# Expert weights split three loads ahead into four buffers, with a light turn's small work tied behind those splits

## The chip, the cores and the metric

One core of a Trainium2 chip runs the whole kernel in one launch. The metric is the device time of that launch in microseconds: 2012.52 us in the median of three runs before the change (2011.22 to 2013.28).

## What is computed

Two layers over 256 latent and 256 context tokens of 1024 features, in float32: a gated linear recurrence with a dense SwiGLU, then windowed attention with a mixture of experts. The change lies in the experts (and touches the attention before them):

```python
logits = (h @ router).astype(jnp.float32)
top_logit, top_idx = lax.top_k(logits, 2)                   # 2 of 8 experts a token
top_w = jax.nn.softmax(top_logit, axis=-1)
gates = jnp.sum(one_hot(top_idx, 8) * top_w[..., None], axis=-2)
for e in range(8):                                          # D_EXPERT = 3584
    g, u = jnp.split(h @ w_gate_up[e], 2, axis=-1)
    out = out + gates[..., e:e + 1] * ((silu(g) * u) @ w_down[e])
```

## The kernel before

A float32 product is made of float32r products: every operand is split into a high and a low part, `split_into` (L112, L113): ACT copies the high part to float32r, then DVE (in places POOL) subtracts it and writes the low part. `mm3` (L127 to L129) multiplies high by high, low by high and high by low.

The experts are worked off one by one, eight **turns** in an order by their number of tokens. Odd turns are **light**: at most 64 tokens, whose high and low parts stand side by side in 128 columns, so that two products for each block of weights do (L1189, L1190); `fold` (L1227) adds the two halves afterwards. Even turns are **heavy**: up to 128 tokens, three products a block. Each turn has 7 **chunks** of 512 hidden features, and a chunk 6 **loads** of weights of 1024 KB: four for gate and up (`up`), two for down (`down`). A load goes through a raw buffer (`raw`, L104: DMA on the SP queue), is split (`weights`) into one `whi` and one `wlo` buffer, and is used by PE. Heavy chunks have 72 large products, light ones 48. The buffers of a kind are used in turn. At the experts there are 11 raw buffers (4 of the stream, 5 of the pool `early`, which the attention also uses as scratch, 1 of the pool `late`, 1 in the free half of `x`) and 3 each of `whi` and `wlo`.

The loop in `run` asks for the gate and up products of a chunk, then for the down products of the chunk before; between the two down loads, `turned` brings this chunk's activations into the layout that its down products need. In a light chunk that is: ACT copies the gate sums and the up sums out of their banks (L1215), PE folds and turns them (L1227), ACT takes the silu (L1229), DVE multiplies (L1230), and the result is split (`eahi`, L112, L113). Each call of `weights` stands where its products are asked for; a scheduler puts the instructions of each engine in an order from that, and each engine works its own queue strictly in order. After a turn, `finished` scales and splits its two sums, and `scatter` adds them to the output (L1266 to L1268); `gather` makes the next turn's tokens (L1137, L1158 for a light turn, L1169 to L1181 for a heavy one).

Ahead of the experts lies the attention's out-projection, whose four loads (`swout`) and one of the experts' first two are split in quarters by ACT and POOL.

## Time and profile before

| | |
|---|---|
| runs, median (range) | 2012.52 us (2011.22 to 2013.28) |
| profiled execution | 2011.05 us, of which the span 2009.3 us |
| mean granted TensorE clock | 0.982 |
| busy: PE, DVE, ACT, POOL | 93%, 76%, 55%, 9% |
| HBM read | 477.10 MB, 238 GB/s over the span |
| experts | from about 980 us to the end |

Busy shares are of one execution. PE's products overlap each other, so that it counts as busy while its rate may be below its best. A row of waits names who waited for whom; idle time of an engine that nobody waits for costs nothing. A window gives what each engine did in a stretch of time.

### The profile page before, as it was taken

To read this page: it belongs to the slowest core of one execution; us is meant where nothing else is said; L and a number is where in the kernel's file an instruction comes from. 1 tells how busy PE (TensorE), PEld (TensorE's weight loads), DVE (VectorE), ACT (ScalarE), POOL (GpSimd) and SP (SyncE) were. 2 spreads that over 40 slices of the span, in tenths; PEclk is the share of its full clock that TensorE was granted. 3 is DMA by queue.
4 is the path that set the end of the run, shared out by engine and by line. 5 is a ranking of instruction groups with operands and counts; after the bars stand their busy time and mean duration, and the time that the engine had idled before them with its cause. 6 is when DMAs were issued, how large, how long until landed. Compare 5 with 4: busy or idle time off the path is not lost.

```text
span 2009.3 us, 29618 instructions
## 1 busy us (share of the span) xinstructions
PE 1874.9 (93%) x11580; PEld 1513.5 (75%) x11580; DVE 1522.9 (76%) x2053; ACT 1114.8 (55%) x1321; POOL 174.3 (9%) x166
## 2 busy tenths in 40 slices
PE   7999999999999999899999988998889988899877
PEld 5888878898888889667878776886668866678655
DVE  4786778596684747775598978888778887788877
ACT  3433332442122224565677877677767767677766
POOL 2233233000000000532100000000000000000000
PEclk8999999999999999898999999999999999999999
DMA  7322223555353432242499999999889999899983
GB/s 267 137 74 96 90 101 127 192 228 188 129 225 128 155 118 75 105 171 104 168 356 351 367 373 342 348 343 342 332 330 348 350 343 338 326 340 353 345 335 118
DMA packets 73811, 480.14 MB, mean 239 GB/s; under 512 B 8768, under 2 KB 11456, under 8 KB 18752
## 3 DMA queue, kind: packets, MB, share of 16 engines
q1 hardware_dynamic: 73664, 478.18, 63.5%
q8 instruction: 93, 1.52, 0.3%
q14 instruction: 54, 0.44, 0.1%
HBM read 477.10 MB, written 1.05 MB: 238 GB/s over the span
## 4 chain that ended last, share of the span: by engine, by line
PE 26%; DVE 13%; ACT 5%; DMA 5%; issue 4%; POOL 0%; DVEq 0%; ACTq 0%
DVE wlo L113 10%; PE ps_a L128 5%; PE ps_a L129 5%; PE ps_a L127 5%; ACT whi L112 4%; DMA raw<-moed 2%; DMA raw<-moegu 2%; PE ps_a L1190 2%; PE ps_b L129 2%; PE ps_b L128 2%; PE ps_b L127 2%; PE ps_a L1189 1%; DVE acc L1268 1%; PE ps_a L1158 1%; PE ps_c L1234 0%
## 5 line engine op out<-in xcount | busy, mean ns | idle before, releaser
L113 DVE TENSOR_TENSOR wlo<-raw,whi 128x2048 fp32r<-128x2048 f32 (+2 forms) x389 | 817.5, 2121 | 143.0 <-ACT whi L112 136.7
L112 ACT ACTIVATE whi<-raw 128x2048 fp32r<-128x2048 f32 (+2 forms) x421 | 703.3, 1690 | 302.6 <-PE ps_a L128 207.0
L129 PE MATMUL ps_a<-hhi,wlo 128*128 128x512 f32 (+1 forms) x800 | 283.8, 355 | 2.1 <-POOL wlo L113 2.1
L127 PE MATMUL ps_a<-hhi,whi 128*128 128x512 f32 (+1 forms) x800 | 283.4, 357 | 0.8 <-ACT hhi L112 0.7
L128 PE MATMUL ps_a<-hlo,whi 128*128 128x512 f32 (+1 forms) x800 | 283.3, 355 | 0.0
L128 PE MATMUL ps_a<-wlo,hhi 128*128 128x512 f32 (+1 forms) x720 | 256.0, 356 | 9.2 <-DVE wlo L113 9.2
L127 PE MATMUL ps_a<-whi,hhi 128*128 128x512 f32 (+1 forms) x720 | 256.3, 356 | 2.3 <-ACT hhi L359 2.0
L129 PE MATMUL ps_a<-whi,hlo 128*128 128x512 f32 (+1 forms) x720 | 253.9, 353 | 2.4 <-DVE hlo L361 2.4
L1190 PE MATMUL ps_a<-wlo,hhi 128*128 128x512 f32 x448 | 186.9, 417 | 46.5 <-DVE wlo L113 46.4
L1189 PE MATMUL ps_a<-whi,hhi 128*128 128x512 f32 x448 | 178.4, 400 | 3.9 <-ACT whi L112 3.9
L129 PEld LDWEIGHTS ps_a<-hhi,wlo 128*128 128x128 f32 x800 | 152.4, 190 | 23.3 <-POOL wlo L113 2.9
L127 PEld LDWEIGHTS ps_a<-hhi,whi 128*128 128x128 f32 x800 | 151.6, 190 | 22.8 <-ACT hhi L112 1.1
L128 PEld LDWEIGHTS ps_a<-hlo,whi 128*128 128x128 f32 x800 | 152.5, 191 | 19.4
L128 PEld LDWEIGHTS ps_a<-wlo,hhi 128*128 128x128 f32 x720 | 136.7, 190 | 31.7 <-DVE wlo L113 14.3
L127 PEld LDWEIGHTS ps_a<-whi,hhi 128*128 128x128 f32 x720 | 136.7, 190 | 25.4 <-issue 2.9
L1190 PEld LDWEIGHTS ps_a<-wlo,hhi 128*128 128x128 f32 x448 | 85.6, 191 | 88.8 <-DVE wlo L113 72.9
L129 PEld LDWEIGHTS ps_a<-whi,hlo 128*128 128x128 f32 x720 | 136.3, 190 | 19.8 <-DVE hlo L361 2.9
L219 DVE SCALAR_TENSOR_TENSOR junk<-raw,crow 128x1024 f32<-128x1024 f32 x80 | 97.7, 1221 | 33.2 <-DMA raw<-wmod1t 32.0
L1189 PEld LDWEIGHTS ps_a<-whi,hhi 128*128 128x128 f32 x448 | 85.8, 191 | 22.1 <-ACT whi L112 6.4
L1190 PE MATMUL ps_b<-wlo,eahi 128*128 128x512 f32 x224 | 85.1, 417 | 16.0 <-DVE wlo L113 15.4
L128 PE MATMUL ps_b<-wlo,eahi 128*128 128x512 f32 x224 | 88.9, 397 | 1.1 <-DVE wlo L113 1.1
L129 PE MATMUL ps_b<-whi,ealo 128*128 128x512 f32 x224 | 87.5, 392 | 0.2 <-DVE ealo L113 0.2
(379 smaller groups left out, 2906.1 us busy)
## 6 DMA issues: line engine op xcount, KB each, us to landing
raw<-moegu SPq DMA_DIRECT2D x202, 1024.0 KB, 6.7
raw<-moed SPq DMA_DIRECT2D x98, 1024.0 KB, 6.9
raw<-wmod SPq DMA_DIRECT2D x26, 1024.0 KB, 5.0
raw<-ffgu SPq DMA_DIRECT2D x22, 1024.0 KB, 4.9
raw<-wmod1t SPq DMA_DIRECT2D x20, 1024.0 KB, 4.8
x<-moegu SPq DMA_DIRECT2D x20, 1024.0 KB, 6.1
raw<-whead SPq DMA_DIRECT2D x14, 768.0 KB, 4.4
x<-moed SPq DMA_DIRECT2D x10, 1024.0 KB, 5.1
```

Of the source, the lines that this page charges most:

```text
L112: self.nc.scalar.activation(hi[:, at], x[:, at], AF.Copy)
L113: (by or self.nc.vector).tensor_tensor(lo[:, at], x[:, at], hi[:, at].bitcast(F32), op=ALU.subtract)
L127: mm(out, l[0], r[0], start=first, stop=False)
L128: mm(out, l[0], r[1], start=False, stop=False)
L129: mm(out, l[1], r[0], start=False, stop=last)
L219: nc.vector.scalar_tensor_tensor(self.junk, w[:, b], 1.0, self.crow[:, who], op0=ALU.mult, op1=ALU.mult, accum_out=self.mod[1][:, 2 * c + ...
L1158: nc.tensor.matmul(g[:, d], l[:, d], r[:, :LIGHT], start=(n == 0), stop=(n == 3))
L1189: nc.tensor.matmul(out, l, r[0], start=first, stop=False)
L1190: nc.tensor.matmul(out, l, r[1], start=False, stop=last)
L1268: nc.vector.scalar_tensor_tensor(acc[:, i, cols], o, gate[:, i, e:e + 1], acc[:, i, cols], op0=ALU.mult, op1=ALU.add)
```

## The change

1. `feed` makes one list of all loads of a run in the order of their use (`chunks`). `take` brings up the list until four loads have been asked for that are not used yet (`ahead=3`), so that three loads beyond the present one have had DMA and split asked for, and hands out the oldest. The first chunk of the first run goes without (`ahead` 0).
2. `split_into` remembers its last two instructions (`made`). `after(n)` ties what is issued in it behind the ACT half of the n-th load ahead, `after(n, True)` behind the DVE half. A light chunk's two copies and its silu come behind the third split ahead, the product of gate and up behind the first, the split of the result behind the third (ACT) and the second (DVE).
3. The last three of these, `finished` and `gather` are kept in a list (`later`), which is worked off within the next `up` behind the first load's products. `folded`, with the fold on PE, comes behind both down loads.
4. Buffers: `early` has 4 instead of 5, `late` is gone, so 9 raw buffers; `whi` and `wlo` have 4 each.
5. In a heavy chunk the silu of the gate sums is asked for before the up products, not after.

```diff
-            self.more(self.pool(self.ctx, "early"), raw=5)
+            self.more(self.pool(self.ctx, "early"), raw=4)
...
-            self.slots["raw"] += [(self.pool(es, "late"), 1), (None, 1)]
-            self.more(self.pool(es, "ahead"), whi=1, wlo=1)
+            self.slots["raw"] += [(None, 1)]
+            self.more(self.pool(es, "ahead"), whi=2, wlo=2)
...
+                def take(ahead=3):
+                    for name, k, at, pieces in islice(todo, max(0, ahead + 1 - len(ready))):
+                        src = ins[name][(FIRST,) + at] if k == 0 else ins[name][(bass.ds(number[k], 1),) + at][0]
+                        with nullcontext() if ahead else tc.issue_after(self.gathered):
+                            ready.append(self.weights(src, 2048, pieces=pieces, loads=pieces) + self.made)
+                    return ready.pop(0)[:2]
+
+                def after(n, low=False):
+
+                    return tc.issue_after(ready[n][2 + low]) if n < len(ready) else nullcontext()
...
                 for j in range(2):
                     for kh in range(2):
-                        ...
-                                w = self.weights(source("moegu", k, c, j, kh), 2048, pieces=at, loads=at)
-                        w = [t.rearrange("p (k n) -> p k n", k=4) for t in w]
+                        w = [t.rearrange("p (k n) -> p k n", k=4) for t in self.take(ahead)]
                         ...
+                        while later:
+                            later.pop(0)()
+                    if light:
+                        with self.after(2):
+                            nc.scalar.copy(out[j], gu[j])
+                    elif j == 0:
+                        nc.scalar.activation(out[0], gu[0], AF.Silu)
...
+            def folded(both):
                 ...
+                with self.after(2):
+                    nc.scalar.activation(a, g, AF.Silu)
+
+                def later():
+                    with self.after(0, True):
+                        nc.vector.tensor_tensor(a, u, a, op=ALU.mult)
+                    with self.after(2):
+                        nc.scalar.activation(out[:, :, :LIGHT], a, AF.Copy)
+                    with self.after(1, True):
+                        nc.vector.tensor_tensor(out[:, :, LIGHT:], a, out[:, :, :LIGHT].bitcast(F32), op=ALU.subtract)
+                return out, later
...
-                        down(pe, pc, pact, y, (0,))
-                        if e < NE:
+                        down(pc, pact, y, (0,))
+                        if e < NE and not light:
                             act = turned(act)
-                        down(pe, pc, pact, y, (1,))
+                        down(pc, pact, y, (1,))
+                        if e < NE and light:
+                            act, rest_of = folded(act)
+                            later.append(rest_of)
```

**ACT, a chunk of a light turn.** Before: the chunk whose gate sums are ps_a_12616 and up sums ps_a_12617. Its loads are 12619 and 12633 (gate), 12647 and 12661 (up); 12677 and 12705 are the down loads of the chunk before.

```order
L112 ACTIVATE whi_12633<-raw_12631 128x2048
L112 ACTIVATE whi_12647<-raw_12645 128x2048
L1215 COPY x_76<-ps_a_12616 128x512
L112 ACTIVATE whi_12661<-raw_12659 128x2048
L112 ACTIVATE whi_12677<-raw_12675 128x2048
L1215 COPY x_76<-ps_a_12617 128x512
L112 ACTIVATE whi_12705<-raw_12703 128x2048
L1229 ACTIVATE x_76<-ps_c_12689 128x256
L112 ACTIVATE whi_12721<-raw_12719 128x2048
L112 ACTIVATE eahi_12690<-x_76 128x4x64
```

After: gate sums ps_a_12625 of the loads 12573 and 12588, up sums ps_a_12626 of 12602 and 12629; 12646 and 12661 are the down loads of the chunk before, 12674, 12689 and 12703 the first loads of the next chunk.

```order
L114 ACTIVATE whi_12629<-raw_12627 128x2048
L1269 ACTIVATE eahi_12615<-x_76 128x4x64
L114 ACTIVATE whi_12646<-raw_12644 128x2048
L1236 COPY x_76<-ps_a_12625 128x512
L114 ACTIVATE whi_12661<-raw_12659 128x2048
L114 ACTIVATE whi_12674<-x_76 128x2048
L1236 COPY x_76<-ps_a_12626 128x512
L114 ACTIVATE whi_12689<-raw_12687 128x2048
L114 ACTIVATE whi_12703<-raw_12701 128x2048
L1263 ACTIVATE x_76<-ps_c_12715 128x256
```

The copy of the gate sums stood one split beyond the last gate load and stands three beyond; so does the copy of the up sums (one beyond 12661 before; 12646, 12661 and 12674 beyond 12629 after).

**PE, the same chunks.** Before, around the fold of the gate sums, within the products of the first up load (ps_a_12617):

```order
L1190 MATMUL ps_a_12616<-wlo_12634,hhi_91 128x512
L1189 MATMUL ps_a_12617<-whi_12647,hhi_91 128x512
L1227 MATMUL ps_c_12689<-fold_9527,x_76 128x64 x4
L1190 MATMUL ps_a_12617<-wlo_12648,hhi_91 128x512
L1189 MATMUL ps_a_12617<-whi_12647,hhi_91 128x512
L1190 MATMUL ps_a_12617<-wlo_12648,hhi_91 128x512
```

After, from the last product of the up sums on; ps_b are the sums of the down products of the chunk before:

```order
L1218 MATMUL ps_a_12626<-wlo_12630,hhi_91 128x512
L1217 MATMUL ps_a_12626<-whi_12629,hhi_91 128x512
L1218 MATMUL ps_a_12626<-wlo_12630,hhi_91 128x512
L1217 MATMUL ps_b_12483<-whi_12646,eahi_12615 128x512
L1217 MATMUL ps_b_12484<-whi_12646,eahi_12615 128x512
L1260 MATMUL ps_c_12715<-fold_9525,x_76 128x64 x4
L1218 MATMUL ps_b_12483<-wlo_12647,eahi_12615 128x512
```

The fold moved from the first up load to the first down load of the chunk before, two loads later.

**POOL, the end of the attention.** L826 and L828 (after: L829, L831) are the two steps of a query norm, of the third and the fourth group of heads here; wlo rows are quarters of weight splits: first eight of the queries' weights, later those of the out-projection and of one load of the experts (four of them before from the buffer in `x`). Before:

```order
L113 TENSOR_TENSOR wlo<-raw,whi 128x512 x8
L826 TENSOR_TENSOR raw<-raw,cst 128x512
L828 TENSOR_TENSOR raw<-raw 128x512
L826 TENSOR_TENSOR raw<-raw,cst 128x512
L828 TENSOR_TENSOR raw<-raw 128x512
L113 TENSOR_TENSOR wlo<-raw,whi 128x512 x8
L113 TENSOR_TENSOR wlo<-x,whi 128x512 x4
L113 TENSOR_TENSOR wlo<-raw,whi 128x512 x8
```

After:

```order
L115 TENSOR_TENSOR wlo<-raw,whi 128x512 x8
L829 TENSOR_TENSOR raw<-raw,cst 128x512
L831 TENSOR_TENSOR raw<-raw 128x512
L115 TENSOR_TENSOR wlo<-raw,whi 128x512 x6
L829 TENSOR_TENSOR raw<-raw,cst 128x512
L115 TENSOR_TENSOR wlo<-raw,whi 128x512
L831 TENSOR_TENSOR raw<-raw 128x512
L115 TENSOR_TENSOR wlo<-raw,whi 128x512 x13
L1027 TENSOR_TENSOR hlo<-yn,hhi 128x4x128
```

Seven quarters of the out-projection's splits moved ahead of the last step of the fourth norm.

## Rows read from the trace of the kernel before

**Rows 1.** The page: busy time of the engines over the whole span (share, instructions).

```profile
PE 1874.9 (93%) x11580; PEld 1513.5 (75%) x11580; DVE 1522.9 (76%) x2053; ACT 1114.8 (55%) x1321; POOL 174.3 (9%) x166
```

**Rows 2.** Instructions of DVE in order of time, the additions of a turn's sums to the output: start us, us, instruction, count. Those after the first and the second turn.

```profile
1129.70 2.73 DVE L1268 SCALAR_TENSOR_TENSOR acc<-ps_a,gate,acc 128x512 f32<-128x512 f32 x4
1254.30 2.72 DVE L1268 SCALAR_TENSOR_TENSOR acc<-ps_a,gate,acc 128x512 f32<-128x512 f32 x4
```

**Rows 3.** Windows between the starts of these additions: stretch, its length, then busy us (instructions) of PE, PEld, DVE, ACT, POOL, the granted clock, DMA share, GB/s. In order: first light turn, second heavy, fourth turn (light), third heavy, sixth turn (light), fourth heavy, last light turn with the end.

```profile
1129.70:1254.30 124.60, 109.68 (x507) 85.51 (x506) 106.61 (x72) 93.83 (x84) 0.00 (x0) 0.97 0.91 356
1254.30:1377.00 122.70, 118.28 (x547) 95.34 (x546) 105.03 (x67) 89.25 (x69) 0.00 (x0) 1.00 0.93 345
1377.00:1513.70 136.70, 114.19 (x520) 86.72 (x520) 109.51 (x73) 96.93 (x85) 0.00 (x0) 0.99 0.87 337
1513.70:1636.00 122.30, 117.89 (x545) 95.01 (x544) 104.59 (x67) 89.08 (x69) 0.00 (x0) 1.00 0.93 344
1636.00:1773.00 137.00, 114.49 (x522) 86.98 (x521) 109.82 (x73) 96.95 (x86) 0.00 (x0) 0.99 0.91 334
1773.00:1896.00 123.00, 118.59 (x548) 95.52 (x548) 104.88 (x65) 89.49 (x70) 0.00 (x0) 1.00 0.93 347
1896.00:2009.30 113.30, 87.45 (x388) 62.34 (x386) 89.25 (x76) 73.06 (x76) 0.00 (x0) 0.98 0.65 241
```

**Rows 4.** ACT in order of time in one chunk of the fourth turn: start us, us, instruction, count, idle time before it and what ended it.

```profile
1403.65 3.71 ACT L112 ACTIVATE whi<-raw 128x2048 fp32r<-128x2048 f32 x2
1410.00 0.58 ACT L1215 COPY x<-ps_a 128x512 f32<-128x512 f32 x1 [2.65 <-PE ps_a L1190]
...
1416.70 0.59 ACT L1215 COPY x<-ps_a 128x512 f32<-128x512 f32 x1 [2.50 <-PE ps_a L1190]
```

**Rows 5.** DVE in order of time in the same chunk, same columns.

```profile
1412.43 4.49 DVE L113 TENSOR_TENSOR wlo<-raw,whi 128x2048 fp32r<-128x2048 f32 x2 [2.20 <-ACT whi L112]
1419.13 2.29 DVE L113 TENSOR_TENSOR wlo<-raw,whi 128x2048 fp32r<-128x2048 f32 x1 [2.21 <-ACT whi L112]
```

**Rows 6.** DMA issues on the SP queue in order of time in the fourth turn: start us, us from the first of the row to the last, what, count. The first four loads of a chunk and of the chunk two later.

```profile
1389.59 9.23 SPq L104 DMA_DIRECT2D raw<-moegu  x4
...
1426.52 9.23 SPq L104 DMA_DIRECT2D raw<-moegu  x4
```

**Rows 7.** Waits from 1000 us to the end: engine, line and tile that waited, for what: us in total, times, longest.

```profile
DVE wlo L113 <- ACT whi L112: 127.5, 100, 2.8
ACT x L1215 <- PE ps_a L1190: 97.8, 42, 3.0
...
DVE wlo L113 <- DMA raw<-moed: 2.1, 1, 2.1
```

**Rows 8.** Groups of instructions from 1010 us on, shapes apart: count | busy us, mean ns of one | idle before, releaser. The splits and a light chunk's small work. Below them two products on PE in order of time (start us, us): the first low product of a gate load and, seven products on, the first of the next load.

```profile
L113 DVE TENSOR_TENSOR wlo<-raw,whi 128x2048 fp32r<-128x2048 f32 x290 | 657.5, 2287 | 123.1 <-ACT whi L112 118.1 <-DMA raw<-moed 2.1 <-DMA raw<-moegu 1.3
L112 ACT ACTIVATE whi<-raw 128x2048 fp32r<-128x2048 f32 x290 | 551.3, 1913 | 62.6 <-PE ps_a L129 33.9 <-PE ps_b L129 18.8 <-PE ps_a L1189 5.6
...
L1215 ACT COPY x<-ps_a 128x512 f32<-128x512 f32 x56 | 32.5, 583 | 97.8 <-PE ps_a L1190 97.8
...
L112 ACT ACTIVATE eahi<-x 128x256 fp32r<-128x256 f32 x28 | 11.6, 413 | 12.7 <-DVE x L1230 12.7
...
L1229 ACT ACTIVATE x<-ps_c 128x256 f32<-128x256 f32 x28 | 10.6, 378 | 11.0 <-PE ps_c L1227 10.9
...
1408.08 0.50 PE L1190 MATMUL ps_a<-wlo,hhi 128*128 128x512 f32 x1 [0.43 <-DVE wlo L113]
...
1409.80 0.39 PE L1189 MATMUL ps_a<-whi,hhi 128*128 128x512 f32 x1
```

**Rows 9.** The same view, the work of gathering a heavy turn's tokens, which a light turn does once.

```profile
L1174 ACT ACTIVATE x<-ps_a,mod 128x128 f32<-128x128 f32 x24 | 9.6, 450 | 0.0
...
L1175 ACT ACTIVATE hhi<-x 128x256 fp32r<-128x256 f32 x12 | 5.1, 425 | 0.1
L1176 DVE TENSOR_TENSOR hlo<-x,hhi 128x256 fp32r<-128x256 f32 x12 | 4.8, 420 | 0.0
...
L1181 ACT ACTIVATE hotT<-ps_c 128x256 fp32r<-128x256 f32 x7 | 2.7, 385 | 0.0
...
L1137 DVE TENSOR_SCALAR hot<-iota,place 128x128 fp32r<-128x128 f32 x6 | 1.4, 280 | 0.0
```

**Rows 10.** Windows (columns as in Rows 3): the beginning of the first light turn, a stretch of the sixth turn, a stretch of a heavy turn.

```profile
1140.00:1170.00 30.00, 28.76 (x142) 23.28 (x142) 30.00 (x18) 27.13 (x23) 0.00 (x0) 1.00 1.00 412
1140.00:1180.00 40.00, 38.41 (x196) 31.51 (x196) 37.15 (x22) 33.56 (x29) 0.00 (x0) 1.00 1.00 414
1650.00:1700.00 50.00, 41.22 (x198) 31.03 (x197) 36.77 (x22) 34.46 (x29) 0.00 (x0) 1.00 0.96 342
1270.00:1350.00 80.00, 80.00 (x380) 66.37 (x379) 67.95 (x41) 59.44 (x47) 0.00 (x0) 1.00 0.95 354
```

**Rows 11.** DMA issues by line: what, count, KB each, median us from issue to landing, for issues from 1140 to 1180 us.

```profile
raw<-moegu SPq DMA_DIRECT2D x10, 1024.0 KB, 8.0
```

**Rows 12.** The end of the attention and the out-projection: a window (columns as in Rows 3), the wait of POOL in 900 to 1000 us (us, times, longest), and the pieces of split on POOL (ns min/median/max, first and last start).

```profile
945.00:960.00 15.00, 12.88 (x102) 11.95 (x103) 5.10 (x8) 8.92 (x22) 10.87 (x8) 1.00 0.36 121
...
POOL wlo L113 <- ACT whi L112: 42.9, 4, 31.6
...
L113 POOL TENSOR_TENSOR wlo<-raw,whi x32: 1257/1292/1829, 805.6 to 965.2; 128x512 fp32r<-128x512 f32 x32
```

More of the change, by code (lines that the diff above doesn't have):

```diff
@@ L996, in experts @@
                 pass
-            early = [self.weights(ins["moegu"][FIRST, 0, 0, kh], 2048, pieces=range(4), by=by) for kh, by in ((0, None), (1, nc.gpsimd))]
+            early = [self.weights(ins["moegu"][FIRST, 0, 0, kh], 2048, pieces=range(4), by=by) + self.made for kh, by in ((0, None), (1, nc.gpsimd))]
             rest = self.x[:, 1].rearrange("p k n -> p (k n)")
@@ L1119, in weigh, with chunks, feed @@
                 number[1:] = nc.values_load_multi_w_load_instructions(ids[0:1, 1:NE], engines=[mybir.EngineType.SP], min_val=0, max_val=NE - 1)[1]
-            def source(name, k, *at):
-                if k == 0:
-                    return ins[name][(FIRST,) + at]
-                return ins[name][(bass.ds(number[k], 1),) + at][0]
+            def chunks(work):
+                for n, (k, c) in enumerate(work + [(NE, 0)]):
+                    last = k == NE - 1 and c == EC - 1
+                    for j in range(2) if k < NE else ():
+                        for kh in range(2):
+                            yield "moegu", k, (c, j, kh), range(4) if last and j else (0,)
+                    for q in range(2) if n else ():
+                        yield "moed", work[n - 1][0], (work[n - 1][1], q), (0, 2, 1, 3) if last or k == NE else (0,)
+            def feed(work, held=()):
+                todo = chunks(work)
+                ready = list(held)
+                for _ in held:
+                    next(todo)
+                def take(ahead=3):
[6 more added lines that the diff above has]
+                    return tc.issue_after(ready[n][2 + low]) if n < len(ready) else nullcontext()
+                return take, after
             self.resident.close()
@@ L1192, in experts, with up @@
             block = lambda x, f: [t[:, f] for t in x] if isinstance(x, (list, tuple)) else x[:, f]
[L1194 removed]
+            def up(xe, ahead, later):
                 gu = [self.bank("a") for _ in range(2)]
+                light = not isinstance(xe, list)
+                out = [spare() for _ in range(1 + light)]
                 for j in range(2):
                     for kh in range(2):
[L1198 to L1204 removed]
+                        w = [t.rearrange("p (k n) -> p k n", k=4) for t in self.take(ahead)]
                         for q in range(4):
@@ L1240, in down @@
+            def down(c, act, y, qs):
                 for q in qs:
-                    at = (0, 2, 1, 3) if k == NE - 1 and c >= EC - 2 else (0,)
-                    w = [t.rearrange("p (k n) -> p k n", k=2) for t in self.weights(source("moed", k, c, q), 2048, pieces=at, loads=at)]
+                    w = [t.rearrange("p (k n) -> p k n", k=2) for t in self.take()]
                     for n in range(2):
@@ L1275, in run, with finish, prepare @@
                 work = [(e, c) for e in range(NE) for c in range(EC)]
-                left, y, due = None, None, None
+                left, y, due, later = None, None, None, []
+                self.take, self.after = feed(work, early)
+                def finish(k, hotT, y):
+                    nonlocal due
+                    due = k, hotT, finished(y)
+                def prepare(k):
+                    nonlocal ready
+                    ready = gather(k, over)
                 for e, c in work + [(NE, 0)]:
                     if c == 0:
-                        now, ready = ready, None
-                    act = up(e, c, now[0], early if (e, c) == (0, 0) else ()) if e < NE else None
-                    if act is not None and not left:
+                        now = ready
+                    if e < NE:
+                        act = up(now[0], 0 if (e, c) == (0, 0) and early else 3, later)
+                    while later:
+                        later.pop(0)()
+                    light = isinstance(act, list)
+                    if not left:
                         act = turned(act)
@@ L1301, in run @@
                         if c == EC - 3 and e < NE - 1:
-                            ready = gather(e + 1, over)
+                            later.append(partial(prepare, e + 1))
+                while later:
+                    later.pop(0)()
                 scatter(*due)
```

48 lines of the change are left out of this document (17 added, 31 removed).

## The prediction

> **What bounds the kernel now.** I read the page first [rows 1]: TensorE (PE) is 93% busy, VectorE (DVE) 76%, ScalarE (ACT) 55%. No engine is the bound of the whole, and the shares mix stages; the experts, from some 980 us on, have two kinds of turn. So I cut it by turns. After a turn its sums are added to the output by four additions on DVE, and the time of these additions marks the turns [rows 2]: 1129.70, 1254.30 and so on. The windows between these marks [rows 3] show the pattern. Heavy turns (the second, fourth and sixth window) take 122.3 to 123.0 us with PE busy 118 of them. Light turns (the third and fifth window) take 136.7 and 137.0 us, though they have only 48 large products a chunk against 72; no engine is full in them: PE 114, DVE 109.5 to 109.8, ACT 97, DMA share 0.87 and 0.91. The first light turn took 124.6.
>
> What fills the light turns is read from one chunk of the fourth turn. ACT [rows 4] splits two loads, waits 2.65 us until PE has done the gate sums, copies them, splits two more, waits 2.50 us for the up sums. DVE [rows 5] needs the high half from ACT, and idles 2.20 and 2.21 us at the same places. The DMA queue [rows 6] repeats two chunks later at a distance of 1426.52 - 1389.59 = 36.93, so 18.46 us a chunk. Of this DVE works 18.46 - 2.20 - 2.21 = 14.05 us. The table of waits over the whole stage agrees [rows 7]: DVE for ACT's split 127.5 us, ACT for the copy 97.8 us. The loop is: PE waits for DVE's low half, ACT waits for PE in order with its next splits queued behind, DVE waits for ACT.
>
> **The change, part by part.**
>
> *Splits three ahead, four buffers.* In the order before, ACT copies gate sums when one split beyond their last load is out; after the change when three are. While ACT then waits for PE, DVE has up to three more low halves to make, 2.29 us each [rows 8], about 6.9 us against a wait of 2.65. Four buffers allow it: split n+4 needs PE to be done with load n, which is about 2 us after DVE finished n (8 products, of which seven steps take 1409.80 - 1408.08 = 1.72 us [rows 8]), and DVE needs split n+4 only three low halves later. ACT's own work in a chunk is 6 x 1.91 + 2 x 0.58 + 0.38 + 0.41 = 13.4 us [rows 8], below 14.05. So in a light chunk DVE becomes the pace and its two idle pieces, 4.4 us, go.
>
> The sum by turns, from DVE's busy time in rows 3. Third and fifth window: idle 136.7 - 109.5 = 27.2 and 137.0 - 109.8 = 27.2. I leave 3 us in each: in the chunk that also gathers the next expert's tokens, ACT has 8 x 0.45 + 4 x 0.43 + 0.39 = 5.7 us more [rows 9], 19.1 in all against DVE's 14.05 plus about 2.2, and that eats the lead. Gain 24 each. First window: 124.6 - 106.6 = 18 idle, of which I leave 3 for the gather and 3 for its beginning, where DVE was already full for 30 us [rows 10]; gain 12. Last turn: idle 113.3 - 89.3 = 24, of which I leave 8 for the last chunk, which is cut into quarters, and for the end, both as before; gain 16. Together 12 + 24 + 24 + 16 = 76 us.
>
> *Heavy turns.* Their work is unchanged. PE is busy all 80 us of a stretch in the second turn [rows 10], and that cover stays: splits, copies and additions lie beside it. Lower end 0; upper end the idle of PE, 122.7 - 118.3 = 4.4, in each of three windows, 13. I take 0, since the stretch is nearest.
>
> *Small work tied behind the splits.* Each tie can hold ACT or DVE: behind the copy of the gate sums waits the next split, behind the copy wait PE's fold products and then the down products of this chunk, which come one chunk later. By the order the fold of the gate sums now stands two loads later, so the products of both up loads cover the copy's 0.58 us. I cost it at nothing; if that cover is gone, each light chunk pays the copy's wait, which is the slower rival below. The loads keep their order on SP; only the out-projection's four now stand ahead of the experts' first.
>
> *Raw buffers 11 to 9.* At the fastest stretch a load took 8.0 us from issue to landing [rows 11]: at 1.0486 MB / 414 GB/s = 2.53 us a load, 3.2 buffers in flight. Nine less those and four under split leaves two, so it costs nothing in the stage. At its start two loads fewer are there when PE begins; lower end 0, upper end 2 x 2.53 = 5.1 us. I take 2, since the queue has the whole first heavy turn to catch up.
>
> *Attention, out-projection.* One scratch buffer fewer; the splits of the out-projection's weights, on POOL, move ahead of the last query's norm. Gain: POOL had waited 31.6 us for a split of these weights, and PE lost 2.1 us between 945 and 960 while POOL made the rest [rows 12], so up to 2 us. Loss: the norm's two POOL steps may wait behind four pieces of 1.29 us, about 5 us. I take 0 and keep -2 to +5.
>
> *Sum.* 76 - 2 = 74 us. The profiled execution took 2011.05 us (span 2009.3), 1.5 below the median of 2012.52. 2011.05 - 74 = 1937; on the median **1938.5**, so I say 1938.
>
> **Can the loads follow?** This is the weak point. 42 loads of 1.0486 MB in 113 us are 390 GB/s. The kernel reached 414 GB/s for 40 us in the first light turn, with DVE full for the first 30 of them [rows 10], so the pace exists. But 342 GB/s at a share of 0.96 between 1650 and 1700 [rows 10] look like a limit of 342 / 0.96 = 356, and rows 3 give 334 / 0.91 = 367 for that turn. I take the 414: landing time was then 8.0 us, so the queue was deeper, and a share near one with few loads in flight says little on what more of them would give. A light turn also starts with buffers full. Against the change speaks the Trainium skill, "DMA: Bandwidth & Descriptors", section "Where 436 GB/s comes from": for HBM to SBUF the HBM side binds at about 358 GB/s a core. By it, 42 loads would take 44.04 MB / 358 GB/s = 123 us as an estimate, the sum would shrink to about 30 us, and 1982 would come out. This trace's 414 GB/s is above that figure; the same page's section "Measured" has a core with an idle neighbour at 425 for 16 MB moved at once (341 for 1 MB), and by the 425 the loads follow.
>
> **The rivals.**
>
> *A. Loads become the pace of the light turns.* For it: the shares of 0.91 and 0.96 in the sixth turn, above [rows 3, 10]. Against: DVE waited 2.1 us for down loads in all this time [rows 7]. At 356 to 367 GB/s a light turn takes 44.04 MB / rate = 123.7 to 120.0 us: gains 1 to 5, 13 to 17, 13 to 17, and 3 to 6 in the last, less 2: 28 to 43, so 1984 to 1970. Landed buffers at the start of a turn are worth up to five loads of 2.9 us, 14 us a turn, and pull it to 1960. Middle 1970.
>
> *B. Nothing is gained.* The lead is never built, because ACT, at 13.4 of 14.05 us, falls back to a split at a time after each gather, and the chunk stays at 18.46. Then 2012 to 2015. Against: 14.05 is reached before in the 30 us of rows 10.
>
> *C. Slower.* The place is ACT in a light chunk: if the split three loads ahead cannot start when PE ends the gate sums (its buffer or its load is late), the copy now stands behind two more splits than before, 2 x 1.91 = 3.8 us, twice a chunk, and the fold and the down products with it. Less the 4.4 us that go, that is 3.2 us in each of 28 light chunks, 90 us: 2102. It decides from the point at which ACT's lead is under two loads for whole turns. Against: DVE's pace leaves ACT 0.6 us of slack in each chunk to build the lead, and each light turn starts behind a heavy one that PE paces, so with the lead full.
>
> **How the numbers follow.** DVE-paced light turns, 1938: 0.68. A, 1970: 0.24. B, 2013: 0.04. C, 2102: 0.04. The likeliest case alone spans 1938 - 13 (heavy turns) - 2 (attention) = 1923 to 1938 + 5 + 3 + some 9 for the three gathers and the handovers = 1955. To hold 8 in 10 the range reaches to most of A: 1918 to 1976. A measurement of this kernel tells 0.2%, some 4 us, from no change. Faster by more: 0.68 + 0.24 + a little of B = 0.93; within: 0.03; slower: 0.04.
>
> **What would show it.** Right: light turns near 112 us in the windows between the additions, with DVE busy over 95% of them; the wait of DVE for ACT's split down from 127.5 to under 50 us; the distance of six issues in a light chunk near 14 to 15 us; DMA near 390 GB/s there; heavy turns unchanged near 122. Case A: DVE's or ACT's wait for raw loads, tens of us, and light turns at 120 or more. Case B or C: the copy's wait for PE as long as before, or PE idle before the fold. My number is wrong if the heavy turns grow, which would mean that they start with empty buffers after a light turn at full rate, or if the attention's end moves by over 5 us.

## The result

The changed kernel took 1933.68 us in the median of four runs (1928.72 to 1935.96), the kernel before, run beside it, 2012.57: a ratio of 0.9605 (95% interval 0.9585 to 0.9626). A second series of the same kernel gave 1933.31 us and 0.9602 (0.9589 to 0.9615). The forecast was 1938.

Busy time on the page after, in place of [rows 1]: the instructions are the same, the span is 82.4 us shorter, and DVE's share has risen from 76 to 79%.

```profile
PE 1849.1 (96%) x11580; PEld 1508.8 (78%) x11580; DVE 1522.8 (79%) x2053; ACT 1103.1 (57%) x1321; POOL 174.9 (9%) x166
```

The additions that marked the turns in [rows 2, 3] no longer do, since they now stand between the splits of the next turn. The start of a turn's first gate product on PE is a better mark, for both kernels. Windows between these starts, before: first light turn, second heavy, second light, and the last light turn with the end (columns as in [rows 3]).

```profile
1103.23:1222.71 119.48, 106.44 (x500) 83.13 (x498) 103.44 (x70) 93.89 (x85) 0.00 (x0) 0.97 0.92 362
1222.71:1350.01 127.30, 123.69 (x568) 100.38 (x566) 110.55 (x70) 92.49 (x69) 0.00 (x0) 1.00 0.93 348
1350.01:1482.04 132.03, 108.72 (x499) 81.63 (x498) 103.91 (x69) 93.62 (x85) 0.00 (x0) 0.99 0.87 333
...
1868.71:2009.30 140.59, 110.73 (x489) 79.51 (x487) 112.20 (x91) 93.22 (x92) 0.00 (x0) 0.99 0.70 260
```

The same of the changed kernel, all seven turns from the first light one on:

```profile
1092.45:1198.67 106.22, 101.35 (x500) 81.04 (x498) 102.14 (x69) 92.02 (x83) 0.00 (x0) 1.00 0.98 394
1198.67:1325.23 126.56, 124.34 (x568) 101.65 (x568) 109.05 (x70) 89.33 (x71) 0.00 (x0) 0.99 0.94 355
1325.23:1436.25 111.02, 103.81 (x500) 80.43 (x498) 104.56 (x69) 93.48 (x84) 0.00 (x0) 1.00 0.99 391
1436.25:1561.34 125.09, 122.89 (x568) 100.41 (x568) 109.06 (x70) 89.33 (x71) 0.00 (x0) 1.00 0.94 359
1561.34:1672.36 111.02, 103.79 (x499) 80.43 (x498) 104.54 (x69) 93.51 (x84) 0.00 (x0) 1.00 0.99 390
1672.36:1798.99 126.63, 124.44 (x568) 101.65 (x568) 108.67 (x68) 89.34 (x71) 0.00 (x0) 0.99 0.94 353
1798.99:1926.90 127.91, 107.73 (x489) 81.93 (x487) 111.43 (x91) 92.17 (x92) 0.00 (x0) 0.96 0.78 303
```

The light turns fell from 119.5, 132.0, 132.0 and 140.6 to 106.2, 111.0, 111.0 and 127.9: 13.3 + 21.0 + 21.0 + 12.7 = 68 us. DVE's work in them is the same (103.9 and 104.6 us in the second one); its idle time is what went. The heavy turns gave 0.7 + 2.2 + 0.7 = 3.6, and the first light turn begins 10.8 us earlier.

One chunk of the second light turn on ACT, in place of [rows 4]: no copy (L1236) waits for PE any more. What waits a little is the copy behind the small work of DVE.

```profile
1381.85 0.59 ACT L1236 COPY x<-ps_a 128x512 f32<-128x512 f32 x1 [0.36 <-DVE eahi L1271]
1382.34 1.92 ACT L114 ACTIVATE whi<-raw 128x2048 fp32r<-128x2048 f32 x1
1384.15 1.90 ACT L114 ACTIVATE whi<-x 128x2048 fp32r<-128x2048 f32 x1
1385.95 0.58 ACT L1236 COPY x<-ps_a 128x512 f32<-128x512 f32 x1
1386.41 3.73 ACT L114 ACTIVATE whi<-raw 128x2048 fp32r<-128x2048 f32 x2
1390.03 0.38 ACT L1263 ACTIVATE x<-ps_c 128x256 f32<-128x256 f32 x1
```

DVE in the same chunk, in place of [rows 5]: one idle piece of 0.32 us instead of two of 2.2.

```profile
1384.29 2.29 DVE L115 TENSOR_TENSOR wlo<-raw,whi 128x2048 fp32r<-128x2048 f32 x1 [0.32 <-ACT whi L114]
1386.50 2.28 DVE L115 TENSOR_TENSOR wlo<-x,whi 128x2048 fp32r<-128x2048 f32 x1
1388.70 4.49 DVE L115 TENSOR_TENSOR wlo<-raw,whi 128x2048 fp32r<-128x2048 f32 x2
```

The issues on SP, in place of [rows 6]: from one pair of down loads to the next 1391.01 - 1376.72 = 14.29 us, against 18.46.

```profile
1376.72 2.54 SPq L106 DMA_DIRECT2D raw<-moed  x2
...
1391.01 2.54 SPq L106 DMA_DIRECT2D raw<-moed  x2
```

The waits from 1000 us to the end, in place of [rows 7]: DVE's wait for ACT's split is down from 127.5 to 57.4 us, the copy's wait for PE (97.8) is gone, and no wait of ACT or DVE for a load is left. One has grown: ACT's split of a light chunk's result waits 44.4 us for DVE's product, 12.7 before [rows 8].

```profile
DVE wlo L115 <- ACT whi L114: 57.4, 67, 2.6
ACT eahi L1269 <- DVE x L1267: 44.4, 24, 3.8
...
ACT x L1236 <- DVE eahi L1271: 5.8, 16, 0.4
```

### The profile page after: what moved, and what is told of

Same layout as the page of the kernel before. It is cut to its first block, busy times and chain, and to the rows that moved or that the text cites. A ratio compares the mean times of both kernels' runs of the same rounds, so it can differ in the third digit from the quotient of the medians.

```text
span 1926.9 us, 29638 instructions
## 1 busy us (share of the span) xinstructions
PE 1849.1 (96%) x11580; PEld 1508.8 (78%) x11580; DVE 1522.8 (79%) x2053; ACT 1103.1 (57%) x1321; POOL 174.9 (9%) x166
## 4 chain that ended last, share of the span: by engine, by line
PE 68%; DVE 18%; ACT 6%; issue 6%; DMA 1%; POOL 1%; DVEq 0%; SPq 0%; ACTq 0%; POOLq 0%
PE ps_a L131 16%; PE ps_a L130 16%; PE ps_a L132 16%; DVE wlo L115 11%; ACT whi L114 4%; PE ps_b L132 2%; PE ps_b L130 2%; PE ps_b L131 2%; PE ps_b L463 1%; PE ps_a L177 1%; PE ps_b L1218 1%; PE ps_c L1260 1%; PE ps_c L540 1%; PE ps_b L1217 1%; DVE acc L1301 1%
## 5 line engine op out<-in xcount | busy, mean ns | idle before, releaser
L115 DVE TENSOR_TENSOR wlo<-raw,whi 128x2048 fp32r<-128x2048 f32 (+2 forms) x382 | 801.2, 2123 | 64.8 <-ACT whi L114 63.2
L114 ACT ACTIVATE whi<-raw 128x2048 fp32r<-128x2048 f32 (+2 forms) x418 | 685.5, 1676 | 260.0 <-PE ps_a L131 209.6
L1218 PE MATMUL ps_a<-wlo,hhi 128*128 128x512 f32 x448 | 181.7, 406 | 17.7 <-DVE wlo L115 15.8
L131 PEld LDWEIGHTS ps_a<-wlo,hhi 128*128 128x128 f32 x720 | 137.2, 191 | 28.9 <-DVE wlo L115 11.5
L222 DVE SCALAR_TENSOR_TENSOR junk<-raw,crow 128x1024 f32<-128x1024 f32 x80 | 97.7, 1222 | 31.8 <-DMA raw<-wmod1t 30.5
L1218 PE MATMUL ps_b<-wlo,eahi 128*128 128x512 f32 x224 | 86.4, 418 | 6.2 <-DVE wlo L115 5.3
L115 DVE TENSOR_TENSOR wlo<-x,whi 128x2048 fp32r<-128x2048 f32 x37 | 84.6, 2286 | 7.5 <-ACT whi L114 7.5
```

The costliest lines, as they stand in the source:

```text
L114: high = self.nc.scalar.activation(hi[:, at], x[:, at], AF.Copy)
L115: low = (by or self.nc.vector).tensor_tensor(lo[:, at], x[:, at], hi[:, at].bitcast(F32), op=ALU.subtract)
L131: mm(out, l[0], r[1], start=False, stop=False)
L222: nc.vector.scalar_tensor_tensor(self.junk, w[:, b], 1.0, self.crow[:, who], op0=ALU.mult, op1=ALU.mult, accum_out=self.mod[1][:, 2 * c + ...
L1218: nc.tensor.matmul(out, l, r[1], start=False, stop=last)
```

## The experiments

All ratios are to the kernel before, run on the same chip in the same series. "Turns" are windows between first gate products; the second light turn stands for the ordinary one (132.0 us before, 111.0 after).

**1. What makes the light turns: buffers, order or ties.**

*Buffers alone*, in the kernel before:

```diff
-            self.more(self.pool(self.ctx, "early"), raw=5)
+            self.more(self.pool(self.ctx, "early"), raw=4)
-            self.slots["raw"] += [(self.pool(es, "late"), 1), (None, 1)]
-            self.more(self.pool(es, "ahead"), whi=1, wlo=1)
+            self.slots["raw"] += [(None, 1)]
+            self.more(self.pool(es, "ahead"), whi=2, wlo=2)
```

> The kernel before with only the buffers of the change: four for each split half, nine raw ones; the order of the experts' code as before. In a light turn ScalarE's order is that of before (the gate copy behind as many splits as there). Theory (the order makes the light turns, the buffers only what lies ahead of them): light turns stay at 119 and 132 us between the first gate products, the stretch before the first light turn shrinks by the 10.8 us that the change showed, about 2002 us. Rival 1 (buffers are the gain: splits run ahead whenever a buffer is free): light turns near 111, 1935 to 1950. Rival 2 (the stretch ahead comes from the changed order of the experts' code): 2012, no change. Rival 3 (two raw buffers fewer cost, as the prediction had it): 2013 to 2017.

Measured: 2016.16 us, ratio 1.0007 (0.9994 to 1.0020). The light turn is 134.3 us, no shorter, so rival 1 falls. The first tokens are gathered 5.9 us earlier than before (970.43 against 976.37): that part does go with the buffers, which speaks against the reason of rival 2, though its time came out. So did the time of rival 3; only 2.8 us of waits for loads stand in this trace from 1000 us on, so the two missing raw buffers are not shown to cost anything. The first light turn starts only 2.1 us earlier, and the profiled execution (2019.17 us, the highest of its twelve) lost 10 us over the turns, which is not explained. Buffers alone gain nothing.

*No ties*, in the changed kernel:

```diff
-                    return tc.issue_after(ready[n][2 + low]) if n < len(ready) else nullcontext()
+                    return nullcontext()
```

> The change without its ties: the splits are written three ahead and have their buffers, but nothing holds the copy, the fold's activations, the products and halves of a light turn behind them. The scheduler then puts the copies where the kernel before had them (as many splits ahead of each). Theory (the place of the copies on ScalarE is the whole mechanism): light turns as before, 119 and 132, only the stretch ahead gains, about 2000 us. Rival (writing the splits ahead with four buffers is enough, the ties are small change): 1935 to 1950.

Measured: 1999.42 us, ratio 0.9932 (0.9919 to 0.9945); light turn 129.05. The theory holds in the main; the 3 us by which this turn is shorter than before are not explained. The splits are written three ahead and have their buffers, yet the waits are those of [rows 7]:

```profile
DVE wlo L115 <- ACT whi L114: 137.1, 99, 2.8
ACT x L1236 <- PE ps_a L1218: 93.7, 40, 2.7
```

The reason is in the order on ACT. In an ordinary light turn the gate copy of a chunk stands behind 256 splits (counted from the kernel's start) in the kernel before, 256 without ties, 258 in the change. The scheduler put the copy back to where it had been; only the tie moves it. No run ties the copies alone, without the silu and the small work of DVE: that the copies are what counts is read from their wait for PE, 97.8 us before, 93.7 without ties, 47.0 and 5.3 with one and two splits ahead (below), none in the change.

*One and two splits ahead*, in the changed kernel (`ahead=1`, ties on that split; the same with 2):

```diff
-                def take(ahead=3):
+                def take(ahead=1):
...
-                        with self.after(2):
+                        with self.after(0):
                             nc.scalar.copy(out[j], gu[j])
```

> The change with its number three set to one: one split ahead, ties on that one, buffers and the deferred small work as in the change. ScalarE's order then has the gate copy one split later than before, the up copy at its old place. Theory (VectorE idles at a copy for as long as ScalarE waits beyond the low halves in hand, and one more low half, 2.2 us, covers one of the two idle pieces): one piece of 2.2 us a light chunk stays, a light turn is about 120 us, and the time 1965 to 1978. Rival (ScalarE needs the whole lead or falls back to a split at a time): light turns near 130, 1995 to 2005. Rival (only buffers or the deferral count): 1934.

> The same with two splits ahead: both copies stand one split later than before, the fold two. Theory: one more low half covers each idle piece of 2.2 us in an ordinary chunk; the gather chunk, where ScalarE has more work, loses 2 to 4 us a turn against three ahead. Light turns 112 to 115, 1937 to 1950. Rival (each split of lead is worth a third of the gain): 1960.

Measured: one ahead 1972.20 us, 0.9797 (0.9783 to 0.9811), light turn 120.8; two ahead 1933.24 us, 0.9607 (0.9593 to 0.9621), light turn 110.3. Both as the theory had it, two ahead even without the loss at the gather. One ahead moves only the gate copy by a split (to 257; the up copy stays at 258), two ahead move both (257 and 259), the change by two (258 and 260). With one ahead half of the copies' wait for PE is left, and DVE keeps one idle piece of 2.0 us a chunk:

```profile
1382.25 6.70 DVE L115 TENSOR_TENSOR wlo<-raw,whi 128x2048 fp32r<-128x2048 f32 x3 [1.99 <-ACT whi L114]
...
1398.62 2.29 DVE L115 TENSOR_TENSOR wlo<-raw,whi 128x2048 fp32r<-128x2048 f32 x1 [2.00 <-ACT whi L114]
```

The window of the second light turn with two ahead shows the same full DVE as with three:

```profile
1332.44:1442.78 110.34, 103.39 (x499) 80.61 (x498) 104.31 (x68) 94.03 (x85) 0.00 (x0) 1.00 0.99 390
```

*Two splits ahead, buffers of before* (three per half, eleven raw):

> Two splits ahead with ties, but with the buffers before: three for each split half, eleven raw. ScalarE's order comes out as that of the change. Theory (the place of the copies on ScalarE counts, three buffers hold two splits ahead): 1930 to 1945, the stretch ahead of the experts as before where the buffers set it. Rival (four buffers are needed: with three, a split ahead waits until PE has done with the load three earlier, so ScalarE stops behind it and the copy with it): 1955 to 1990.

Measured: 1939.52 us, 0.9627 (0.9611 to 0.9643); light turn 110.4. Three buffers of each half do, with eleven raw ones; four are not needed. Three beside nine raw ones were not run. The turns from the first light one on are as long as with four buffers (832.5 us against 831.0). What is lost lies ahead: the first gather is at 978.42, the first light turn at 1107.53.

*Nothing deferred* (ties and lead as in the change; `rest_of`, `finish` and `prepare` called at once, not put into `later`):

```diff
-                            later.append(rest_of)
+                            rest_of()
-                        later.append(partial(finish, pe, phot, y))
+                        finish(pe, phot, y)
-                            later.append(partial(prepare, e + 1))
+                            prepare(e + 1)
```

> The change with splits three ahead and ties, but the second half of a light chunk's small work, the finishing of an expert's sums and the gather of the next expert's tokens stand where the kernel before had them, not after the next load's products. Theory (the place of the copies is nearly all; the deferral keeps VectorE's finishing products and the gather's activations from standing ahead of a split while they wait for TensorE): light turns 2 to 4 us longer, 1935 to 1955. Rival (the deferral is half of the gain): 1965 to 1980. Rival (it does nothing): 1928 to 1936.

Measured: 1932.75 us, 0.9584 (0.9566 to 0.9602); light turn 110.8. My theory was wrong here and the last rival right: the deferral does nothing that can be measured.

**2. What paces a light turn now.**

*Fewer loads*, in the changed kernel (a light chunk's second down load splits the first's raw tile again):

```diff
-        r = self.raw(src, n, loads) if raw is None else raw
+        r = self.held = self.raw(src, n, loads) if raw is None else raw
...
+                            again = self.held if name == "moed" and at[1] and k % 2 and pieces == (0,) else None
-                            ready.append(self.weights(src, 2048, pieces=pieces, loads=pieces) + self.made)
+                            ready.append(self.weights(src, 2048, pieces=pieces, loads=pieces, raw=again) + self.made)
```

> The change, but in the light turns the second down load of a chunk is left out and the first one's tile is split twice: 40 or so loads a light turn instead of 48, the splits and products all there. Theory (VectorE's low halves pace a light turn): no change, light turns 109 to 112, 1925 to 1937, at a rate of 325 to 335 GB/s. Rival (loads pace it, at the 391 to 394 GB/s of the change): eight loads of 2.7 us fewer, light turns near 92 to 100, 1870 to 1890.

Measured: 1917.03 us, 0.9511 (0.9491 to 0.9531), between the two. (A light turn has 42 loads, not 48, and 36 were issued in this one.) The windows part the two: the second light turn took 109.8 us, as the theory said, at 350 GB/s. The heavy turn before it fell by 5 us, counted from its second gate product on; its first, at 1199.30, stands ahead of the last down products here:

```profile
1204.99:1326.54 121.55, 121.55 (x567) 100.59 (x567) 107.45 (x70) 88.66 (x70) 0.00 (x0) 1.00 0.94 350
...
1326.54:1436.33 109.79, 102.39 (x501) 80.96 (x500) 105.20 (x69) 94.60 (x85) 0.00 (x0) 1.00 0.92 350
```

So loads don't pace a light turn; the heavy turns are looked at in part 4.

*No low halves in light turns* (`wlo` is the `whi` tile, DVE's subtraction left out there):

> The change, but in the light turns no low half is made (its products run with the high half), so VectorE has next to nothing to do there; loads, ScalarE's work and the products are all there. Theory (VectorE paces): the next limit is ScalarE, 6 splits at 1.82, two copies at 0.48 and 0.58 for the rest, 12.4 us a chunk against 14.29: light turns 98 to 104, 1885 to 1905, at 420 GB/s and more. Rival (loads are at their limit at 391 to 394): light turns stay at 111, 1930. Rival (the loads stop at the 440 that an ordinary chunk of the change shows, or at 414): light turns 100 to 106.

Measured: 1887.53 us, 0.9375 (0.9360 to 0.9391). With DVE free the light turn falls to 97.7 us, shorter than expected, and PE is busy 96.9 us of it:

```profile
1317.38:1415.04 97.66, 96.91 (x491) 81.29 (x490) 18.13 (x29) 90.72 (x83) 0.00 (x0) 1.00 1.01 421
```

The loads followed at 421 GB/s, and no engine waited for one. DVE's low halves are the pace of the changed kernel's light turns, 111.0 - 97.7 = 13.3 us each above the next limit, which is not the loads.

*One low half in six on GpSimd*:

```diff
+                            by = nc.gpsimd if name == "moed" and at[1] and k % 2 and pieces == (0,) else None
-                            ready.append(self.weights(src, 2048, pieces=pieces, loads=pieces) + self.made)
+                            ready.append(self.weights(src, 2048, pieces=pieces, loads=pieces, by=by) + self.made)
```

> The change, but in the light turns the low half of one load in six (the second down load of a chunk) is made by GpSimd, which is idle there. Theory (VectorE paces): VectorE's chunk falls from 13.97 to 11.8 us, ScalarE's 12.4 to 12.8 is next, light turns 98 to 104, 1885 to 1905. GpSimd needs some 5.2 us for it (four pieces of 1.29) and has a lead of three loads, so nothing waits for it. Rival (GpSimd and VectorE slow each other, or GpSimd's half comes late): light turns at 111 or more, 1930 to 1960.

Measured: 1987.11 us, 0.9861 (0.9834 to 0.9889): slower than the change, and than the rival's 1960, light turn 123.9. The theory of the pace is not touched, but my use of it failed, for the reason that the rival gave. GpSimd's half in one chunk:

```profile
1404.45 4.57 POOL L115 TENSOR_TENSOR wlo<-raw,whi 128x2048 fp32r<-128x2048 f32 x1 [12.04 <-ACT whi L114]
```

and DVE's next low half:

```profile
1406.15 5.02 DVE L115 TENSOR_TENSOR wlo<-x,whi 128x2048 fp32r<-128x2048 f32 x1 [2.12 <-ACT whi L114]
```

It starts while GpSimd works and ends at 1411.17, 2.15 us after GpSimd's end at 1409.02: about its own 2.29 us, begun when GpSimd had done. In all 23 such pairs of the light turns VectorE's half ends 2.15 us after GpSimd's. The Trainium skill, "SBUF — State Buffer", section "Who interferes with whom", has an exclusive lock on the ports that the two share, and a VectorE instruction with two inputs from SBUF contend with a GpSimd one that reads SBUF; these rows agree. So GpSimd gave 2.29 us and took 2.73 here (2.3 in the mean of the 23), and it came late besides: PE waited 51.1 us in all for its halves.

**3. The stretch ahead of the light turns.** The changed kernel once more, for a second profile:

> The changed kernel itself, for a second profile. Theory (of the 10.8 us that the first profile gained ahead of the first light turn, some 3 belong to the buffers and the rest to TensorE's clock, granted at 1.00 between 970 and 990 us there and at 0.74 to 0.78 in five others with the same code up to there): the first light turn's gate products begin at 1098 to 1101 where that stretch is at 0.74 to 0.78, and near 1092 where it is at 1.00; time 1928 to 1936. Rival (the 10.8 us are the change's own): 1092 to 1093 whatever the clock.

Measured: 1933.31 us; span 1932.9; the first light turn starts at 1099.93. Its turns are as long as in the first profile (106.2, 126.6, 111.0, 125.1, 111.0, 125.1, 128.0), so the 6.0 us between the spans lie ahead of them, within 1.5 us. Windows of 970 to 980 us in the first profile, then in the second (granted clock in the third column from the right):

```profile
970.00:975.00 5.00, 5.00 (x33) 4.50 (x33) 2.06 (x5) 4.09 (x12) 0.00 (x0) 1.00 0.00 0
975.00:980.00 5.00, 5.00 (x24) 4.14 (x23) 5.00 (x3) 4.93 (x4) 0.00 (x0) 1.00 0.39 131
```

```profile
970.00:975.00 5.00, 5.00 (x25) 5.00 (x25) 1.57 (x4) 2.83 (x8) 0.00 (x0) 0.50 0.01 3
975.00:980.00 5.00, 5.00 (x18) 4.24 (x18) 2.68 (x3) 2.23 (x7) 0.00 (x0) 0.51 0.00 0
```

In both PE had been busy 3.57 of the 5 us before. In the second, 10 us then ran at the lower level of the clock (0.50, which is 1.2 GHz), which is 5 us of work; in the first none did. A second dip, of 1.7 us of work, follows 50 us later in the second profile alone; first profile, then second:

```profile
1020.00:1025.00 5.00, 5.00 (x23) 3.90 (x22) 2.95 (x4) 3.12 (x3) 0.00 (x0) 1.00 1.01 419
```

```profile
1020.00:1025.00 5.00, 5.00 (x15) 3.95 (x16) 3.42 (x4) 1.25 (x2) 0.00 (x0) 0.66 1.02 429
```

The theory holds: 3.3 us of the 10.8 remain in this execution, and the two dips are 6.7 of the 7.5 us between the two starts. The other profiles with these nine raw buffers and the changed order line up: the first light turn starts at 1091.85 where neither dip is there (no low halves), at 1094.48 with the second alone (one ahead), and at 1098.71 to 1101.59 with both.

**4. The handover to a heavy turn, and a faster version.** In the changed kernel, DVE at the start of the second heavy turn:

```profile
1205.70 2.28 DVE L115 TENSOR_TENSOR wlo<-raw,whi 128x2048 fp32r<-128x2048 f32 x1
1209.95 0.69 DVE L1240 TENSOR_TENSOR x<-ps_a,x 128x512 f32<-128x512 f32 x1 [1.97 <-PE ps_a L132]
```

and PE shortly after:

```profile
1212.89 0.50 PE L1218 MATMUL ps_b<-wlo,eahi 128*128 128x512 f32 x1 [0.33 <-DVE wlo L115]
1216.91 0.62 PE L131 MATMUL ps_a<-wlo,hhi 128*128 128x512 f32 x1 [1.83 <-DVE wlo L115]
```

It is the stall of [rows 4, 5] on another engine: DVE waits in order for PE's sums with low halves queued behind, and PE then waits for these. Tied as in the light turns:

```diff
-                        nc.scalar.activation(out[0], gu[0], AF.Silu)
+                        with self.after(2):
+                            nc.scalar.activation(out[0], gu[0], AF.Silu)
...
-                        self.mark = nc.vector.tensor_tensor(out[0], gu[1], out[0], op=ALU.mult).ins
+                        with self.after(2, True):
+                            self.mark = nc.vector.tensor_tensor(out[0], gu[1], out[0], op=ALU.mult).ins
```

> The change, and in a heavy turn the gate's silu on ScalarE and the product with it on VectorE are tied behind the splits two further on as well. In the change the first such product of a heavy turn stands on VectorE behind the low half of the second down load, waits 1.97 us for TensorE's up sum with the next low halves queued behind it, and TensorE then waits 0.33 and 1.83 us for these low halves, at each of the three handovers from a light turn to a heavy one. In the run with fewer loads the product stood two low halves later, without a wait, and its heavy turns took 121.4 to 121.6 us against 125.1 to 126.6. Theory (this place is the handover's loss): heavy turns 121.5 to 123.5, 1918 to 1926. Rival (fewer loads made those heavy turns short): 125 to 127, no change. Rival (two low halves later is too late for the transposes of the product): TensorE waits for them, heavy turns longer, 1935 to 1960.

Measured: 1931.50 us, 0.9591 (0.9578 to 0.9604), 1.8 us below the change run beside it, with intervals that overlap; the time of the theory, 1918 to 1926, was missed. The windows show why:

```profile
1205.32:1327.91 122.59, 122.54 (x564) 99.99 (x564) 110.28 (x69) 88.41 (x69) 0.00 (x0) 1.00 0.95 369
1327.91:1440.77 112.86, 103.94 (x503) 80.89 (x502) 103.13 (x69) 94.17 (x85) 0.00 (x0) 1.00 0.96 381
```

The heavy turn is 4.0 us shorter (2.5 in the two others, both against the second profile), as expected, and PE waits no more; the light turn behind it is 1.8 us longer. At that turn's start DVE waited 2.24 us for ACT's split of the heavy result and 2.64 for PE's down sums.

The second of these waits goes when the finishing product is tied too, on top of the above:

```diff
-                    nc.vector.tensor_tensor(yg, y[n], gf[:, n * NT:(n + 1) * NT], op=ALU.mult)
+                    with self.after(1, True):
+                        nc.vector.tensor_tensor(yg, y[n], gf[:, n * NT:(n + 1) * NT], op=ALU.mult)
```

> The ties of heavy turns as in the run before, and the finishing product of an expert's sums on VectorE tied two low halves later than there. At the start of a light turn this product stood on VectorE ahead of a low half and waited 2.64 us for TensorE's down sums. Theory (VectorE paces a light turn, so its idle pieces there are the light turn's time): 2 to 2.7 us from each of the light turns that follow a heavy one, against the run with heavy ties alone; 1921 to 1928. Rival (the sums' two banks come free later and TensorE's next down products wait for them): no change or slower, 1930 to 1945.

Measured: 1926.06 us (1925.23 to 1926.75), 0.9569 (0.9556 to 0.9582), as expected: 7 us below the change in the medians, and the intervals of the ratios to the kernel before don't overlap. It beats both kernels. The light turn is back, and shorter:

```profile
1205.72:1328.73 123.01, 122.77 (x564) 99.99 (x564) 110.10 (x69) 88.51 (x69) 0.00 (x0) 1.00 0.94 367
1328.73:1438.88 110.15, 103.16 (x504) 81.13 (x502) 103.05 (x69) 94.15 (x85) 0.00 (x0) 1.00 0.98 391
```

## Why the prediction was right, and where its steps were not

**The mechanism was right.** An in-order wait on ACT held back splits that DVE had to have, and with the copies further back DVE paces the light turns. One split more ahead of a copy covers one idle piece: two idle pieces of 2.2 us a chunk (18.46), one (one ahead, 16.37), none (two or three ahead, 14.29) gave light turns of 132.0, 120.8 and 110.3 to 111.0 us. The forecast's signs were met: six issues in 14.3 us, 391 GB/s, no waits for loads. DVE's wait for ACT, 57.4 us, missed the "under 50" a little, and DVE was busy 94 to 96% of a light turn (87% of the last), not over 95% in each.

**Light turns, 76 forecast, 68 measured.** The term was too large by 8. (The two go by different marks, so a few us of the 8 may belong to the heavy turns beside them.) I left DVE 3 us of idle time in a middle turn; it kept 111.0 - 104.6 = 6.4. Of that, 2.7 us is the wait at the turn's start for PE's down sums, which I hadn't looked for, and 3.6 are waits for ACT's split, around the gather. In the last turn the gain was 12.7, not 16.

**Where the gain was put was wrong.** I gave it to "splits three ahead, four buffers" and costed the ties at nothing. The runs part these: without ties 1999, with buffers alone 2016, with ties and three buffers at two ahead 1940. The ties are the gain; writing the splits ahead gives them something to be tied to, and the fourth buffer (at two ahead, with eleven raw ones) and the deferral are worth nothing in the light turns. The step that failed is "in the order before ... after the change when three are": that order comes from the ties, and I read it off the new order without asking which part of the change made it.

**The stretch ahead, 2 us of loss forecast.** It gained 10.8 us in the first profile and 3.3 in the second. The out-projection's term, 0 with at most 2 us of gain, was too small: the first gather came 8.2 and 7.0 us earlier (at 968.16 and 969.35 against 976.37), 5.9 with the buffers alone, and 2.0 later with the buffers of before. It goes with the buffers: with four of each half, GpSimd's last pieces of these weights ended at 951.8 us (second profile) instead of 966.4, and the wait of 22.3 us of its fourth norm's step for PE, with those pieces queued behind, is gone: the step starts behind other pieces without a wait. Against that, [rows 12] had told me only of 31.6 us in which GpSimd waited for ACT, and that wait stayed (35.4). How much of the 7 to 8 us this order of the pieces is worth stays open, for the clock differs there too. Before, and then in the second profile of the change:

```profile
905.00:910.00 5.00, 5.00 (x24) 3.33 (x20) 2.33 (x10) 3.43 (x10) 1.35 (x2) 0.51 0.28 120
915.00:920.00 5.00, 5.00 (x10) 2.28 (x11) 4.45 (x17) 3.65 (x11) 0.00 (x0) 0.67 0.61 210
```

```profile
905.00:910.00 5.00, 4.40 (x32) 2.78 (x31) 4.65 (x19) 3.16 (x8) 0.00 (x0) 1.00 0.79 333
915.00:920.00 5.00, 5.00 (x46) 3.49 (x44) 3.71 (x16) 4.26 (x12) 0.00 (x0) 1.00 0.00 0
```

Over 900 to 925 us that is up to 6.8 us of PE's work. With two ahead and the buffers of before the clock was at 0.50 to 0.86 there as well, from 905 to 930; with the buffers alone and in both profiles of the change it was at 1.00. Whether the buffers spared it, by sparing PE waits, is not shown. Some 7 us between the two profiles are the dips after 970 us, which one execution has and another has not; the kernel before had 3.4 us of them, between 975 and 985. What the two missing raw buffers cost at the start could not be seen beside that.

**Heavy turns, 0 forecast, 3.6 and 5.2 measured** in the two profiles: the size was near, and within the bound of 13. Which part of the change made them shorter was not separated. Not foreseen was the handover, a wait of the same kind one engine on; its ties were worth 2.5 to 4 us a heavy turn, half of which the light turns gave back until the finishing product was tied as well.

**The sum was near partly by luck.** The 8 us too many in the light turns were made up by the 3.6 to 5.2 of the heavy turns and the stretch ahead, which came out 5.3 to 12.8 better than forecast.

**The rivals.** C, the copy behind more splits, did not come: no copy waits for PE any more. A had the loads bind at 356 to 367 GB/s. They ran at 391 in the light turns of the change and at 421 in those without low halves. Taking the 414 GB/s of [rows 10] rather than the share of 0.96 was right: the share read 0.99 at 391 GB/s and 1.01 at 421, so it doesn't tell how near the limit is. The Trainium skill, "DMA: Bandwidth & Descriptors", section "Where 436 GB/s comes from", has the HBM side bind at about 358 GB/s for a core; with one core at work these windows are above that.

## What to carry to other kernels

When an engine works strictly in order, look in its queue for an instruction that waits for another engine, and count what stands behind it that a third engine needs: moving it back by as many instructions as cover its wait was nearly the whole gain here, and more lead or more buffers added nothing. Where a scheduler orders the queue, writing work earlier may change nothing; compare the resulting order, and tie what has to stay behind. After such a fix look for the same pattern one engine on, and in the stretch behind a gain, where it may be given back.

## What the runs showed of the hardware

- GpSimd and VectorE did not work side by side on these subtractions: a VectorE low half of 2.29 us took 5.02 us beside a GpSimd one of 4.57 us, and in all 23 pairs of that run it ended 2.15 us after GpSimd's.
- TensorE's clock fell to its lower level for 10 us behind a wait of 1.43 us for VectorE (ahead of the first gather) in one execution of a kernel and not in another, with the same work before; that alone is 5 us of difference between their spans.
- In a light turn without low halves, loads of 1024 KB moved 41.1 MB in 97.7 us, 421 GB/s, with 11.5 to 12.1 us from issue to landing (7.1 to 7.5 in the change's second light turn, at 391).
